# A hybrid encoder trunk on one core: the last pass of each attention score tile on 128 rows instead of 64, and a limit of nine on the fetched tiles of the state-space units

## The chip, the cores and the metric

One Trainium2 chip, one core of it. The metric is the device time of one launch in microseconds (us); lower is better. Engines are called by the profile's names: PE is TensorE (its matmuls), PEld its weight loads, DVE VectorE, ACT ScalarE, POOL GpSimd, SP SyncE, which only issues DMAs here.

## What is computed

Two post-norm layers on 512 tokens of 1024 channels, in f32. The even layer has a convolution branch (31 taps), a latent attention branch with 8 heads and a cross-attention branch; the odd layer has a state-space branch (S5, two directions, 64 groups of 16 channels) and a cross-attention branch. The part of the reference that the score tiles compute:

```python
def one_block(args):
    qn_b, qr_b = args
    s = (jnp.einsum('bqhd,bkhd->bhqk', qn_b, k_nope).astype(jnp.float32)
         + jnp.einsum('bqhr,bkr->bhqk', qr_b, k_rope).astype(jnp.float32)) * scale
    p = jax.nn.softmax(s, axis=-1).astype(v.dtype)
    return jnp.einsum('bhqk,bkhd->bqhd', p, v)
```

`q_rope` and `k_rope` have 64 components, `q_nope` and `k_nope` 128. The part that the state-space units compute, for each direction:

```python
bu_re = jnp.einsum('bsgc,gpc->bsgp', u, bb_re)
bu_im = jnp.einsum('bsgc,gpc->bsgp', u, bb_im)
_, _, x_re, x_im = lax.associative_scan(
    _cplx_combine, (a_re_seq, a_im_seq, bu_re, bu_im), reverse=reverse, axis=1)
return (jnp.einsum('bsgp,gcp->bsgc', x_re, c_re.astype(f32))
        - jnp.einsum('bsgp,gcp->bsgc', x_im, c_im.astype(f32)))
```

## The kernel before

**Numbers in two parts.** A large f32 operand is split into a high part (rounded by a cast on ACT) and a low part (the rest, by a subtraction on DVE), and a product is three matmul passes: high by high, low by high, high by low. Tiles of such parts are of the type float32r and lie in the arena `sr`; f32 tiles lie in `sb`, small ones in `sz`, PSUM is `ps`. A pass of 512 columns reads as `ps<-sr 128*128 128x512`, where the first pair is rows by columns of the weights.

**Heads (`mla_head`, L900).** Each of the eight heads makes four score tiles of 128 queries by 512 keys, each of five passes into one PSUM bank: three for the 128 components without rotary, two for the 64 rotary ones. For the rotary part the query tile `st` holds on 128 rows both the high part and the low part of the head's 64 rows (the even head has the high part on rows 0 to 63, the odd head on rows 64 to 127). `krh` and `krl` are the high and the low part of the rotary keys; both have the 64 keys' rows twice, on rows 0 to 63 and 64 to 127. So the fourth pass, `st` by `krh` on 128 rows, gives high by high and low by high at once. The fifth pass takes the high rows of `st` alone, by the same 64 rows of `krl` (L924, L934).

**Units (`s5_unit`, L1293).** Layer 1 has eight units of eight groups each. A unit fetches from DRAM its input `U` (128x512) and six tiles of 128x1024 words, in this order: two with its input matrices (`B`, L1304), one with rotations (`E`, L1305), two with output matrices (`C`, L1357) and one strip of the direct term (`Tt`, L1359). On PE come eight matmuls into halves of a bank (`64x256` below, the z passes; each reads in the trace as two), eight transposes (`128x128`), then 24 matmuls for the output (`64x128`): for each quarter two of the direct term and four by the states `X`. Between the transposes and the states DVE makes six products, four scans of 511 elements (`64x511`) and four products; POOL combines those into `X[0]` and `X[1]` (L1355, L1356). Between the units PE has the passes of other work: gates, the cross-attention's heads and, after the last, the matmuls of the gated unit and the output projection.

**The planner.** The program records every operation of both layers and then schedules them itself (`schedule`, L289), with costs for each instruction, due times by program order, and an allocator for the arenas and the PSUM banks (`alloc`, L361). The result is one fixed order for each engine. An operation is placed once its inputs are ready by the planner's costs and its tiles have room. `QUOTA` (L65) says how many tiles of a tag may live at once; a tag without an entry is limited by the arena alone (21504 words for `sb`). The tag of a `pair()` without a name is its line, so before the change the six fetched tiles of a unit all have the tag of L1298, with no entry. To a matmul the planner gives the same cost for the same columns, whatever its rows (L262):

```python
return 13.0 + on * 0.4175
```

All instructions are issued from one line, L535, so the trace is read by shape and arena.

Of the kernel before, what the change touches and what calls it, by code (L numbers as in the profile page):

```python
# [61 lines left out]

SB_WORDS = {"S": 21504, "R": 26624, "Z": 4864}
ENGINES = ("PE", "DVE", "ACT", "POOL", "SP")
QUOTA = dict(wr=3, wh=4, wl=4, wrv=1, whv=1, wlv=1, wrk=1, whk=1, wlk=1, A=4, S=3, T=2, R=1, Q=1, O=4, V=1, Z=2, W=2, Y=1, pr=6, bb=2, bt=2, nat=2, ncim=2, strips=2, qE=1, qt=2, qbt=1, qpw=1, qC=2, qB=1, C=2, D=1, cgl=2, U=2)  # L65
INF = float("inf")
NEAR, RESERVE = 30, dict(R=3584, S=2048)
RESERVEP = dict(R=4096, S=2560)
# [111 lines left out]
class Prog:  # L180
# [108 lines left out]
    def schedule(self):  # L289
# [71 lines left out]
        def alloc(o, near):  # L361
            done = []
            ok = True
            for x in o.tiles:
                if x.space == "D" or x.off is not None:
                    continue
                q = QUOTA.get(x.tag)
                if nxt.get(x.tag, 0) != x.idx or (q and live.get(x.tag, 0) >= q):
# [169 lines left out]
class Kernel:  # L538
# [361 lines left out]
    def mla_head(self, h):  # L900
        nc, A = self.nc, self.A
        if h % 4 == 0:
            self.v = self.mla_v(h // 4)
        wkn = self.wload(A["wkn"][h], 256, tag="k")
        ckv = [(t[0][:], t[1][:]) for t in self.ckv]
        cqa = lambda k: (self.cq[k][0][:], self.cq[k][1][:])
        ps = self.bank("A")
        self.mm3(ps[:], [self.wk(wkn, k) for k in range(2)], ckv)
        kh, kl = self.split(ps[:])
        ps = self.projF(A["wqn"][h], cqa, 6)  # L910
        qh, ql = self.split(ps[:])
        if h % 2 == 0:
            ps = self.projF(A["wqr"][h // 2], cqa, 6)
            r = self.rope(ps)
            self.stk = []
            for i in range(2):
                st = self.big(F32R)
                a, b = slice(i * 64, i * 64 + 64), slice((1 - i) * 64, (1 - i) * 64 + 64)
                nc.scalar.copy(st[a], r[a])
                nc.vector.tensor_tensor(st[b], r[a], st[a].bitcast(F32), op=ALU.subtract)  # L920
                self.stk.append(st)
        i = h % 2
        st = self.stk[i]
        rows = slice(i * 64, i * 64 + 64)  # L924
        scale = 192.0 ** -0.5
        pr = []
        for t in range(4):
            sl = slice(t * P, (t + 1) * P)
            s = self.bank("S")
            nc.tensor.matmul(s[:], lhsT=qh[:, sl], rhs=kh[:], start=True, stop=False)  # L930
            nc.tensor.matmul(s[:], lhsT=ql[:, sl], rhs=kh[:], start=False, stop=False)
            nc.tensor.matmul(s[:], lhsT=qh[:, sl], rhs=kl[:], start=False, stop=False)
            nc.tensor.matmul(s[:], lhsT=st[:, sl], rhs=self.krh[:], start=False, stop=False)
            nc.tensor.matmul(s[:], lhsT=st[rows, sl], rhs=self.krl[rows], start=False, stop=True)  # L934
            mx = self.sm(1, tag="mx")
            nc.vector.reduce_max(mx[:], s[:], axis=AX.X)
            p = self.big(F32, "pr")
            self.softmax_tail(s[:], p[:], scale, mx[:])
            pr.append(p)
        pt = []  # L940
        for k in range(4):
            tp = self.bank("T")
            for t in range(4):
                nc.tensor.transpose(tp[:, t * P:(t + 1) * P], pr[t][:, k * P:(k + 1) * P], self.ident[:])
            pt.append(self.split(tp[:]))
        o = self.bank("V")
        vs = slice((h % 4) * P, (h % 4) * P + P)
        self.mm3(o[:], [(v[0][:, vs], v[1][:, vs]) for v in self.v], [(a[:], b[:]) for a, b in pt])
        m = self.tmp()
        nc.sync.dma_start(out=m[:], in_=self.mgd[h][:])  # L950
        nc.vector.scalar_tensor_tensor(m[:], o[:], 0.5, m[:], op0=ALU.mult, op1=ALU.mult)
        return m
# [340 lines left out]
    def s5_unit(self, i):  # L1293
        nc, A = self.nc, self.A
        V, G = nc.vector, nc.gpsimd

        def load(src, t=None):
            t = t or self.pair()  # L1298
            nc.sync.dma_start(out=t[:], in_=src)
            return t  # L1300

        half = lambda t, x: t[:, x * N:(x + 1) * N]
        U = load(self.ud[i][:].rearrange("s (c n) k -> (s c) (n k)", n=8), self.big())
        B = [load(self.s5d[2 * i + h][0][:]) for h in range(2)]  # L1304
        E = load(self.rotd[i][:])  # L1305
        E = [half(E, x) for x in range(2)]

        zt = []
        for j in range(2):
            zp = self.bank("W")  # L1310
            for m in range(2):
                for h in range(2):
                    n = j * 4 + m * 2 + h
                    nc.tensor.matmul(zp[h * 64:h * 64 + 64, m * 256:m * 256 + 256].rearrange("p (x c) -> p x c", x=2),
                                     lhsT=U[:, n * 64:n * 64 + 64],
                                     rhs=B[j][:].rearrange("p (x c) -> p x c", x=2)[:, :, (n % 4) * P:(n % 4) * P + P],
                                     start=True, stop=True, skip_group_check=True)
            t = self.big()
            nc.scalar.copy(t[:], zp[:])
            zt.append(t)  # L1320
        Z = [self.bank("Z"), self.bank("Z")]
# [11 lines left out]
        t = [self.tmp() for _ in range(2)]  # L1333
# [6 lines left out]
        W = Z  # L1340
# [9 lines left out]
        t = [self.tmp() for _ in range(2)]  # L1350
# [6 lines left out]
        C = [load(self.s5d[2 * i + h][1][:]) for h in range(2)]  # L1357
# [3 lines left out]
        Y = self.bank("Y")  # L1361
# [262 lines left out]
```

## Time and profile before

| | |
|---|---|
| median of 3 runs | 1063.86 us (1058.15 to 1064.89) |
| the profiled execution | 1060.0 us, span 1058.2 us |
| mean granted TensorE clock | 0.979 |
| PE busy | 1007.6 us (95%), 5296 matmul records |
| PEld busy | 792.2 us (75%) |
| DVE busy | 799.2 us (76%) |
| ACT busy | 450.1 us (43%) |
| POOL busy | 514.7 us (49%) |
| DMA | 180.02 MB, mean 170 GB/s |

Times in the rows are microseconds from the start of the span; a row of a timeline merges neighbouring instructions of one kind, and names the shape of its first one. Matmuls are pipelined and their listed lengths overlap, so a matmul's pace is read from a run of them. "<-" names whose semaphore ended a wait. The stages: the even layer's projections up to about 355 us, the eight heads to about 553 (the convolution's taps on DVE run beside both), the even layer's output projection and the odd layer's first projections to about 690, the state-space units to about 875, then the gated unit and the last projection.

### The profile page before, as it was taken

To read this page: it belongs to the slowest core of one execution; us is meant where nothing else is said; L and a number is where in the kernel's file an instruction comes from. 1 tells how busy PE (TensorE), PEld (TensorE's weight loads), DVE (VectorE), ACT (ScalarE), POOL (GpSimd) and SP (SyncE) were. 2 spreads that over 40 slices of the span, in tenths; PEclk is the share of its full clock that TensorE was granted. 3 is DMA by queue.
4 is the path that set the end of the run, shared out by engine and by line. 5 is a ranking of instruction groups with operands and counts; after the bars stand their busy time and mean duration, and the time that the engine had idled before them with its cause. 6 is when DMAs were issued, how large, how long until landed. Compare 5 with 4: busy or idle time off the path is not lost. (4 is left out here: it accounts for less than half of the span.)

```text
span 1058.2 us, 15020 instructions
## 1 busy us (share of the span) xinstructions
PE 1007.6 (95%) x5296; PEld 792.2 (75%) x5296; DVE 799.2 (76%) x1285; ACT 450.1 (43%) x798; POOL 514.7 (49%) x741
## 2 busy tenths in 40 slices
PE   9999899999999999998799999999989979999996
PEld 7888788787788666665578888887767757888885
DVE  7787999999999898987896648517797695434346
ACT  5532455555323457475672223423436344422210
POOL 0557767788899988888699901000121011000001
PEclk9999999999999999998899999999999998999998
DMA  7433634325776454445398753883856633243413
GB/s 261 140 116 114 209 115 168 127 95 173 261 234 220 132 169 135 133 139 197 130 307 257 248 194 120 308 268 120 242 188 198 242 107 104 96 139 120 149 50 79
DMA packets 80171, 180.02 MB, mean 170 GB/s; under 512 B 24161, under 2 KB 28897, under 8 KB 80097
## 3 DMA queue, kind: packets, MB, share of 16 engines
q1 hardware_dynamic: 80096, 179.07, 51.9%
q8 instruction: 41, 0.67, 0.3%
q14 instruction: 34, 0.27, 0.1%
HBM read 142.93 MB, written 36.11 MB: 169 GB/s over the span
## 5 line engine op out<-in xcount | busy, mean ns | idle before, releaser
L535 PE MATMUL ps<-sr 128*128 128x512 f32 (+1 forms) x3904 | 925.5, 392 | 28.4 <-DVE sr L535 13.0
L535 PEld LDWEIGHTS ps<-sr 128*128 128x128 f32 x3904 | 709.9, 190 | 201.3 <-issue 21.7
L535 DVE TENSOR_TENSOR sr<-sb,sr 128x1024 fp32r<-128x1024 f32 (+4 forms) x230 | 270.1, 1186 | 172.4 <-ACT sr L535 130.2
L535 POOL TENSOR_TENSOR sb<-sb 128x512 f32<-128x512 f32 (+3 forms) x246 | 256.2, 1055 | 190.9 <-DVE sb L535 177.7
L535 ACT CAST sr<-sb 128x1024 fp32r<-128x1024 f32 (+4 forms) x230 | 200.7, 886 | 323.9 <-PE ps L535 187.2
L535 DVE SCALAR_TENSOR_TENSOR ps<-sb,sz,ps 128x503 f32<-128x503 f32 (+14 forms) x240 | 167.5, 736 | 0.0
L535 POOL TENSOR_TENSOR sz<-sz 128x64 f32<-128x64 f32 (+2 forms) x75 | 44.4, 596 | 221.6 <-DVE sz L535 218.2
L535 POOL TENSOR_TENSOR sb<-sb,sz 128x512 f32<-128x512 f32 (+4 forms) x160 | 131.8, 842 | 31.1 <-DVE sz L535 11.2
L535 ACT CAST sr<-ps 128x512 fp32r<-128x512 f32 (+1 forms) x100 | 55.8, 570 | 45.5 <-PE ps L535 45.2
L535 DVE TENSOR_TENSOR sr<-ps,sr 128x512 fp32r<-128x512 f32 (+1 forms) x100 | 65.3, 661 | 10.7 <-ACT sr L535 9.8
L535 ACT COPY sb<-ps 128x512 f32<-128x512 f32 (+3 forms) x78 | 40.8, 541 | 73.0 <-PE ps L535 51.9
L535 DVE SCALAR_TENSOR_TENSOR sb<-sb,ps 128x512 f32<-128x512 f32 x64 | 47.1, 739 | 29.6 <-ACT sb L535 12.5
L535 PE MATMUL ps<-sz,sb 128*128 128x128 f32 (+2 forms) x608 | 62.4, 237 | 4.1 <-DVE sr L535 1.8
L535 PE MATMUL ps<-sb 128*64 128x128 f32 (+2 forms) x768 | 58.4, 306 | 8.0 <-POOL sb L535 7.5
L535 PEld LDWEIGHTS ps<-sz,sb 128*128 128x128 f32 (+1 forms) x608 | 47.1, 131 | 20.8 <-ACT sb L535 6.8
L535 PEld LDWEIGHTS ps<-sb 128*64 128x64 f32 (+1 forms) x768 | 36.4, 131 | 33.3 <-POOL sb L535 13.1
L535 POOL TENSOR_TENSOR sb<-sz 64x64 f32<-64x64 f32 (+1 forms) x128 | 55.3, 440 | 4.9
L535 ACT ACTIVATE sb<-ps 128x512 f32<-128x512 f32 (+1 forms) x72 | 38.1, 548 | 41.1 <-PE ps L535 38.8
L535 ACT ACTIVATE sb<-ps,sz 128x256 f32<-128x256 f32 (+1 forms) x64 | 36.8, 580 | 18.6 <-DVE sz L535 13.6
L535 DVE TENSOR_TENSOR sb<-sb,ps 128x512 f32<-128x512 f32 x63 | 40.4, 680 | 2.0 <-PE ps L535 1.3
L535 DVE TENSOR_TENSOR_SCAN ps<-sb,ps 64x511 f32<-64x511 f32 x32 | 39.2, 1224 | 1.8 <-ACT ps L535 1.1
L535 ACT ACTIVATE sb<-sb,sz 128x512 f32<-128x512 f32 (+1 forms) x65 | 38.2, 622 | 5.3 <-DVE sz L535 5.2
(47 smaller groups left out, 338.9 us busy)
## 6 DMA issues: line engine op xcount, KB each, us to landing
sb<-w SPq DMA_DIRECT2D x70, 512.0 KB
sb<-scr SPq DMA_DIRECT2D x48, 512.0 KB
scr<-sb SPq DMA_DIRECT2D x40, 512.0 KB
sb<-scr SPq DMA_DIRECT2D x76, 256.0 KB
sb<-wo SPq DMA_DIRECT2D x32, 512.0 KB
scr<-sb SPq DMA_DIRECT2D x46, 256.0 KB
sb<-s5bt SPq DMA_DIRECT2D x16, 512.0 KB
sb<-wglu SPq DMA_DIRECT2D x16, 512.0 KB
```

What stands on the lines that cost most here:

```text
L535: o.ins = getattr(eng[o.eng], o.meth)(*[real(x) for x in o.a], **{k: real(v) for k, v in o.k.items()})
```

## The change

The fifth pass of each score tile runs on all 128 rows of `st` and `krl`. It so adds the product of the low parts, which the reference's full product contains too. And the fetched tiles of the units get a tag of their own, `un`, with an entry of nine in `QUOTA`.

```diff
-QUOTA = dict(wr=3, ..., cgl=2, U=2)
+QUOTA = dict(wr=3, ..., cgl=2, U=2, un=9)
...
         i = h % 2
         st = self.stk[i]
-        rows = slice(i * 64, i * 64 + 64)
         scale = 192.0 ** -0.5
...
             nc.tensor.matmul(s[:], lhsT=st[:, sl], rhs=self.krh[:], start=False, stop=False)
-            nc.tensor.matmul(s[:], lhsT=st[rows, sl], rhs=self.krl[rows], start=False, stop=True)
+            nc.tensor.matmul(s[:], lhsT=st[:, sl], rhs=self.krl[:], start=False, stop=True)
...
         def load(src, t=None):
-            t = t or self.pair()
+            t = t or self.pair("un")
             nc.sync.dma_start(out=t[:], in_=src)
             return t
```

Up to the middle of the units each engine's order is as before; from there on layer 1 is in another order on all five engines. In the rows below `128x512` is a pass of other work, `64x256` a z pass, `128x128` a transpose, `64x128` an output matmul (two of the direct term come first, then the states').

PE around the last unit, before: its z passes are done, its transposes are the row of eight, and the 20 outputs behind them belong to the unit before.

```order
L535 MATMUL ps<-sr 128x512 x19
L535 MATMUL ps<-sb 64x128 x2
L535 MATMUL ps<-sz,sb 128x128 x8
L535 MATMUL ps<-sr 128x512 x3
L535 MATMUL ps<-sb 64x128 x20
L535 MATMUL ps<-sr 128x512 x4
L535 MATMUL ps<-sb 64x128 x2
L535 MATMUL ps<-sr 128x512 x4
L535 MATMUL ps<-sb 64x128 x2
L535 MATMUL ps<-sr 128x512 x5
```

The same place now: the last of the unit's z passes, its two direct terms, its transposes, and its first state outputs behind the row of 53.

```order
L535 MATMUL ps<-sb 64x256 x4
L535 MATMUL ps<-sb 64x128 x2
L535 MATMUL ps<-sr 128x512 x8
L535 MATMUL ps<-sz,sb 128x128 x8
L535 MATMUL ps<-sr 128x512 x53
L535 MATMUL ps<-sb 64x128 x2
L535 MATMUL ps<-sr 128x512 x5
L535 MATMUL ps<-sb 64x128 x20
```

The outputs of the unit before the last now come ahead of the last unit's transposes, and the passes of other work between those and the first state output went from 3 + 4 + 4 to 53.

DVE in the last unit now: six products, with a split (`sr<-sb,sr`) among them, then the scans (the order lists a scan as SCALAR_TENSOR_TENSOR) and the four products.

```order
L535 TENSOR_TENSOR ps<-sb,ps 128x512
L535 TENSOR_TENSOR sb<-sb,ps 128x512
L535 TENSOR_TENSOR sr<-sb,sr 128x512
L535 TENSOR_TENSOR ps<-sb,ps 128x512
L535 TENSOR_TENSOR sb<-sb,ps 128x512
L535 TENSOR_TENSOR ps<-sb,ps 128x512
L535 SCALAR_TENSOR_TENSOR ps<-sb,ps 64x511
L535 TENSOR_TENSOR ps<-ps,sb 128x512
L535 SCALAR_TENSOR_TENSOR ps<-sb,ps 64x511 x3
L535 TENSOR_TENSOR sb<-sb,ps 128x512 x4
```

Before, the six products of the last unit stood together, as the trace shows them.

PE at the fifth and sixth unit now: the first row of 20 is the fifth unit's outputs, the z passes and the transposes are the seventh's, the other rows of `64x128` the sixth's.

```order
L535 MATMUL ps<-sb 64x128 x20
L535 MATMUL ps<-sr 128x512 x2
L535 MATMUL ps<-sb 64x128 x2
L535 MATMUL ps<-sr 128x512 x7
L535 MATMUL ps<-sb 64x256 x8
L535 MATMUL ps<-sz,sb 128x128 x3
L535 MATMUL ps<-sb 64x128 x2
L535 MATMUL ps<-sz,sb 128x128 x5
L535 MATMUL ps<-sr 128x512 x5
L535 MATMUL ps<-sb 64x128 x20
```

Rows of this form stood at the third and fourth unit before.

SP, the fetches of the fourth unit, the two orders' difference: `128x1x1024` is the strip, `w` a weight tile, `128x512` the next unit's input.

```order
 L535 DMA sb<-scr_3367 128x1024
 L535 DMA sb<-scr_3573 128x1024
+L535 DMA sb<-w 128x1024 x2
 L535 DMA sb<-scr_3622 128x1x1024
-L535 DMA sb<-w 128x1024 x3
-L535 DMA sb<-scr_5945 128x512
+L535 DMA sb<-w 128x1024
+L535 DMA sb<-scr_5942 128x512
```

The strip, the last of a unit's six tiles, went behind two weight tiles.

## Rows read from the trace of the kernel before

**Rows 1.** Stages: length, busy us of PE, PEld, DVE, ACT, POOL; PEclk, DMA share, GB/s

```profile
355.00:414.00 59.00, 55.67 (x305) 37.04 (x305) 52.43 (x101) 35.65 (x73) 50.30 (x69) 1.00 0.46 144
414.00:448.00 34.00, 31.66 (x179) 24.38 (x178) 32.63 (x46) 18.77 (x36) 29.07 (x34) 1.00 0.45 139
448.00:482.00 34.00, 30.02 (x177) 19.89 (x175) 28.07 (x58) 25.00 (x52) 30.93 (x42) 1.00 0.41 129
482.00:553.00 71.00, 61.16 (x291) 42.13 (x291) 58.44 (x91) 42.06 (x78) 57.01 (x70) 0.86 0.66 216
553.00:690.00 137.00, 136.47 (x730) 113.52 (x730) 85.11 (x99) 45.09 (x61) 59.73 (x63) 0.99 0.69 228
690.00:875.00 185.00, 173.56 (x1102) 131.58 (x1100) 133.74 (x189) 78.42 (x172) 22.20 (x24) 0.99 0.61 192
875.00:1058.00 183.00, 174.03 (x794) 143.61 (x794) 83.21 (x113) 50.01 (x72) 5.07 (x5) 0.97 0.34 107
```

**Rows 2.** Groups by shape, PE, whole span: count, busy us, mean ns, idle before

```profile
L535 PE MATMUL ps<-sr 128*128 128x512 f32 x3584 | 877.6, 399 | 26.8 <-DVE sr L535 11.8 <-DVE sb L535 7.1 <-ACT sb L535 4.5
...
L535 PE MATMUL ps<-sr 64*128 64x512 f32 x32 | 17.3, 542 | 0.0
```

**Rows 3.** Timeline of PE, three runs: start, length, shape of the first, count

```profile
339.82 10.13 PE L535 MATMUL ps<-sr 128*128 128x512 f32 x44
...
366.23 2.70 PE L535 MATMUL ps<-sr 64*128 64x512 f32 x8
...
495.33 6.68 PE L535 MATMUL ps<-sr 128*128 128x512 f32 x11 [1.15 <-DVE sr L535]
```

**Rows 4.** Groups by shape, PE, of 366.3:368.7, then of 495.4:501.4

```profile
L535 PE MATMUL ps<-sr 64*128 64x512 f32 x2 | 1.0, 494 | 0.0
...
L535 PE MATMUL ps<-sr 64*128 64x512 f32 x3 | 2.4, 791 | 0.0
```

**Rows 5.** Groups by shape, PE, of 355:414, then of 482:553

```profile
L535 PE MATMUL ps<-sr 64*128 64x512 f32 x16 | 7.9, 495 | 0.0
...
L535 PE MATMUL ps<-sr 64*128 64x512 f32 x8 | 5.4, 681 | 0.0
```

**Rows 6.** DVE's waits for PE in 355:414, 448:482, 482:553: us, times, longest

```profile
DVE sz L535 <- PE ps L535: 3.7, 7, 0.9
...
DVE sb L535 <- PE ps L535: 1.8, 2, 1.3
DVE sz L535 <- PE ps L535: 1.5, 1, 1.5
...
DVE sr L535 <- PE ps L535: 3.2, 2, 2.8
...
DVE sz L535 <- PE ps L535: 1.8, 4, 0.6
```

**Rows 7.** Timeline of PE at the last unit's first state outputs, waits in brackets

```profile
873.97 0.69 PE L535 MATMUL ps<-sb 128*64 128x128 f32 x4 [5.63 <-POOL sb L535]
875.05 2.50 PE L535 MATMUL ps<-sr 128*128 128x512 f32 x5 [0.39 <-DVE sr L535]
```

**Rows 8.** Busy time by stage, behind that wait

```profile
875.00:881.00 6.00, 5.95 (x39) 5.01 (x41) 0.00 (x0) 0.00 (x0) 1.12 (x1) 0.50 0.01 3
```

**Rows 9.** Timeline of DVE, the last unit's first product

```profile
862.61 0.70 DVE L535 TENSOR_TENSOR ps<-sb,ps 128x512 f32<-128x512 f32 x1
```

**Rows 10.** Timeline of PE at the third to fifth unit, waits in brackets

```profile
783.30 1.08 PE L535 MATMUL ps<-sb 128*64 128x256 f32 x8
784.92 1.08 PE L535 MATMUL ps<-sb 128*64 128x256 f32 x8 [0.53 <-DVE ps L535]
...
786.83 0.33 PE L535 MATMUL ps<-sz,sb 128*128 128x128 f32 x1 [0.46 <-DVE sb L535]
787.58 0.44 PE L535 MATMUL ps<-sb 128*64 128x128 f32 x4 [0.42 <-POOL sb L535]
```

**Rows 11.** Timeline of SP, fetches from DRAM scratch: start, length of the burst, count

```profile
776.63 4.92 SPq L535 DMA_DIRECT2D sb<-scr  x7
```

More of the change, by code (lines that the diff above doesn't have):

```diff
@@ L64 @@
 ENGINES = ("PE", "DVE", "ACT", "POOL", "SP")
-QUOTA = dict(wr=3, wh=4, wl=4, wrv=1, whv=1, wlv=1, wrk=1, whk=1, wlk=1, A=4, S=3, T=2, R=1, Q=1, O=4, V=1, Z=2, W=2, Y=1, pr=6, bb=2, bt=2, nat=2, ncim=2, strips=2, qE=1, qt=2, qbt=1, qpw=1, qC=2, qB=1, C=2, D=1, cgl=2, U=2)
+QUOTA = dict(wr=3, wh=4, wl=4, wrv=1, whv=1, wlv=1, wrk=1, whk=1, wlk=1, A=4, S=3, T=2, R=1, Q=1, O=4, V=1, Z=2, W=2, Y=1, pr=6, bb=2, bt=2, nat=2, ncim=2, strips=2, qE=1, qt=2, qbt=1, qpw=1, qC=2, qB=1, C=2, D=1, cgl=2, U=2, un=9)
 INF = float("inf")
```

## Prediction

> **What bounds the kernel now.** I read the busy time by stage first. From 553 us to the end PE is the bound: 136.47 of 137 us ahead of layer 1's state-space units, 173.56 of 185 us while they run, 174.03 of the last 183 [rows 1]. Before that, in the eight attention heads (355 to 553), PE is busy 55.67 of 59, 31.66 of 34, 30.02 of 34 and 61.16 of 71 us, and DVE nearly as long: 52.43, 32.63, 28.07 and 58.44 [rows 1]. There the two wait for each other. So PE can gain in two places: from passes in the heads that take longer than they need, and from the 11.4 us in which it stands in the units' stage (185 less 173.56). The change touches both: the score's last pass in the heads, and the number of fetched tiles in the units.
>
> **Edit 1, the last score pass on 128 rows.** 32 passes (8 heads, 4 query tiles) are on 64 rows. Their listed mean is 542 ns against 399 for a 128-row pass of the same 512 columns [rows 2], but listed times overlap, so I take whole runs. A run of 44 passes on 128 rows takes 10.13 us [rows 3]. Less the last one's own 0.40, that is 9.73 / 43 = 0.226 us a pass. A run of eight takes 2.70 us [rows 3] and holds two 64-row passes [rows 4]. Eight at the plain pace would take 7 x 0.226 + 0.40 = 1.98, so the two cost 0.72 more, 0.36 us each.
>
> From 482 to 553 the granted clock is 0.86 on the mean [rows 1], and a 64-row pass takes 681 ns on the mean against 495 in the first stage [rows 5]. A run of eleven there takes 6.68 us [rows 3], with three 64-row passes of 791 ns [rows 4]. At the lower of the two clocks the plain pace is 0.452, eleven take 4.97, and the overhang of a run's last pass (0.40 - 0.226 = 0.17, at most doubled) makes it 5.14 to 5.32. So three cost 1.36 to 1.54, and I take 0.50 each. Of the eight passes in this stage (681 - 495) / (791 - 495) = 0.63 are at the lower clock: five at 0.50 and three at 0.36, 3.6 us. The first 16 [rows 5] cost 16 x 0.36 = 5.8, the other eight, in the third stage, 2.9. The sum is 12.3 us of PE. After the edit each costs as much as its neighbours: nothing more is loaded or evicted, since both operands have 128 rows already.
>
> How much of it reaches the end? The order in the heads is unchanged on every engine, so DVE must come earlier too, and it can do so only by time in which it waited for PE. In the first stage its small operations waited 3.7 us for PE, against 5.8 saved; in the third 1.8 + 1.5 = 3.3 against 2.9; in the last 3.2 + 1.8 = 5.0 against 3.6 [rows 6]. In the second DVE is full (32.63 of 34 [rows 1]) and merely carries the shift on. So 3.7 + 2.9 + 3.6 = 10.2 is the most that I expect, and I take 9.0, which leaves 1.2 for waits that PE newly has for DVE. From 553 on PE is full, and what is gained stays gained. Bounds: 12.3 if DVE gives way everywhere, 3.6 if all of the first 24 passes' gain is eaten.
>
> What the rows show is that a pass on half the rows costs more than a whole one [rows 2 to 4]. The Trainium skill, "TensorE: Matmul & The Clock Gate", section "Part 2: What happens when you issue a matmul", says of the weight load that the row count does not matter, and of a stream of matmuls that its pace is set by the columns alone; by that edit 1 saves nothing, and the sum is edit 2 alone. The Trainium skill, "TensorEngine Tiling (Array Packing)", section "Tiling Modes", says that a change of tiling mode drains the engine; with that the trace agrees, at 0.36 us a pass.
>
> **Edit 2, at most nine fetched tiles.** No instruction is added on any engine. The planner places layer 1 anew from the middle of the units on, and two places count.
>
> The last unit. Before, between its transposes and its first state output PE has 3 + 4 + 4 passes of 512 columns and the unit before's outputs, and then stands 5.63 us for POOL and 0.39 for DVE [rows 7]. Right behind that the granted clock is 0.50 for 6.00 us, in which PE is busy 5.95 [rows 8]: half, 3.0 us, is lost. After, 53 passes stand there, 53 x 0.226 = 12.0 us. What they must cover is the unit's chain on DVE and POOL: from 862.61, DVE's first product [rows 9], to 873.97, when PE goes on [rows 7], 11.4 us. In the new order one more DVE operation on 128x512 stands within it, 0.70 by that first product's row [rows 9]. So 12.0 of cover for a chain of 12.1: I take 0.5 us of wait. Should the cover be gone, it costs up to those 12.1.
>
> The fifth and sixth unit now follow each other as the third and fourth did before, where PE stood 0.53 + 0.46 + 0.42 = 1.4 us [rows 10]. That place moves, and I cost the move at nothing. But the seventh unit's z passes, which stand between those two, come soon after its tiles are fetched, since only nine may be there. Before, the fifth unit was in that position: a burst of seven fetches was issued from 776.63 on [rows 11], and its z passes began at 783.30 with no wait ahead of the first [rows 10]. I take 1.0 us for the new place; the bounds are 0 and the whole of that stretch, 783.30 - 776.63 = 6.7 us. The weights' fetches, which SP issues in the same queue, now go partly ahead of a unit's strip tile; they are needed earlier, and I cost that at nothing, or at the same 6.7 if the strip is late.
>
> Sum of edit 2: 5.63 + 0.39 + 3.0 - 0.5 - 1.0 = 7.5. Bounds: 9.0 with no new wait; 9.0 - 6.7 - 6.0 = -3.7 with a late burst and two more falls of the clock at 3.0 each.
>
> **The sum.** 9.0 + 7.5 = 16.5 us. The profiled execution took 1060.0, so 1043.5. The median of the runs is 1063.9, 3.9 above that execution; against the median I expect 1047.4, given as 1047, or 1.6% faster. A change of 1%, 10.6 us, is about what a measurement of this kernel can tell from none.
>
> **Rivals.**
> Edit 1 is eaten: PE's shorter passes become PE's waits, because DVE has as little as 4% of slack. For it: DVE busy 32.63 of 34 us in the second stage [rows 1]. Against it: DVE's own waits for PE, 12.0 us in the rows named [rows 6]. Time: 1063.9 - 7.5 = 1056.4. That half the rows cost no more than all would end at the same number, and rows 3 and 4 leave it little. By the skill's rule on rows, above, it would be so.
>
> Edit 2 only moves the wait: the tight pair or the last unit's cover costs what was won. For it: 12.1 of chain against 12.0 of cover. Against it: 53 passes where 11 stood. Time: 1063.9 - 9.0 = 1054.9.
>
> Slower: with nine tiles a unit fetches only half of its successor's six ahead, so that fetches are late unit after unit. The place is each unit's first z pass; the price is a burst of 6.7 us [rows 10, 11] and the clock's 3.0 behind it [rows 8], 9.7 a unit. Two late units use up the gain (19.4 against 16.5), and three give 1063.9 - 16.5 + 29.1 = 1076.5. Against it: before, one unit's fetches were as late, without a wait, and DMA is busy only 0.61 of this stage [rows 1].
>
> **Chances.** Both terms as summed, 0.58 (own range 1041 to 1053). Edit 1 eaten, 0.14, and rows that cost nothing, 0.03. Edit 2 moved, 0.14. Slower by late fetches, 0.07. Neither gains, 0.04. Faster by over 1% (under 1053.2) is the first case and 0.08 of the two rivals that lie next to that border, 0.66; slower by over 1% is 0.07; within 1% the rest, 0.27. The range: at best 12.3 + 9.0 = 21.3, which is 1042.6 against the median and, as the fastest run shown lies 5.7 under it, some 1038; at worst 3 us of gain, 1061, which takes in the rivals next to the border and leaves the slow one out.
>
> **What would show it.** Edit 1 is right if no 64-row pass of 512 columns is left, runs in the heads go at 0.226 us a pass, and the stage that began at 553 begins some 9 us earlier. It is eaten if PE's waits in the heads grow by what its busy time falls. Edit 2 is right if PE's longest wait in the units is under 2 us and the granted clock stays at 1.00 through the last unit. It is wrong if PE waits over 3 us for a DMA, DVE or POOL at the z passes of the fifth or seventh unit or at any unit's state outputs. More than 1061 would mean that both terms failed, or that a new stall of over 10 us stands among the units.

## The result, and the profile after

The changed kernel takes 1051.70 us in the median of 3 runs (1050.03 to 1053.27), against 1063.86: a ratio of 0.9898, interval 0.9867 to 0.9929. Timed again beside 23 runs of the kernel before, it came to 0.9902 (0.9868 to 0.9936). It is faster by 1%, at the border that the forecast set between faster and the same: its first median lies 1.5 us below that border (1053.2), its second, 1055.29, 2.1 us above. The forecast was 1047 us, 1.6%.

The profiled execution took 1050.0 us, span 1048.2, which is 10.0 less than before. The trace was cut at the same instruction of PE as the kernel before at 355.6 and 552.7 us: the heads now take 191.2 us for 197.1 (6.0 less, before rounding), all that follows 501.5 for 505.5 (4.0 less), and what lies ahead is alike. The busy time by stage, cut to within half a microsecond where [rows 1] is cut (columns as there):

```profile
355.00:411.00 56.00, 51.58 (x305) 37.25 (x305) 53.15 (x102) 36.29 (x74) 51.25 (x69) 1.00 0.48 153
411.00:446.00 35.00, 32.81 (x176) 25.32 (x177) 32.81 (x45) 18.31 (x35) 28.78 (x34) 0.95 0.43 133
446.00:479.00 33.00, 28.46 (x179) 20.98 (x177) 27.75 (x59) 25.80 (x54) 31.36 (x44) 0.96 0.45 142
479.00:547.00 68.00, 56.16 (x290) 40.97 (x289) 58.43 (x89) 41.00 (x77) 55.11 (x68) 0.89 0.68 217
547.00:684.00 137.00, 136.34 (x729) 113.52 (x729) 84.28 (x99) 44.95 (x61) 59.75 (x63) 0.99 0.69 227
684.00:865.00 181.00, 173.09 (x1092) 129.99 (x1092) 127.72 (x181) 76.64 (x168) 20.53 (x22) 1.00 0.62 201
865.00:1048.00 183.00, 173.47 (x806) 142.37 (x804) 90.13 (x122) 51.70 (x77) 6.48 (x6) 0.99 0.33 104
```

The first stage is 3 us shorter, the second 1 longer at a clock of 0.95 where [rows 1] had 1.00, the third 1 shorter at 0.96 for 1.00, the fourth 3 shorter, the units 4. PE's largest group by shape over the whole span:

```profile
L535 PE MATMUL ps<-sr 128*128 128x512 f32 x3616 | 881.2, 398 | 30.1 <-DVE sr L535 12.5 <-DVE sb L535 8.3 <-ACT sb L535 4.6
```

and in PE's timeline the run of eight that [rows 3] has at 366.23:

```profile
364.99 2.10 PE L535 MATMUL ps<-sr 128*128 128x512 f32 x8
```

All 64-row passes of 512 columns are gone: 3584 + 32 = 3616. The run of eight takes 2.10 us for 2.70, 0.30 for each of its two. PE's idle time ahead of these passes rose from 26.8 [rows 2] to 30.1. PE's timeline at the last unit's first state outputs:

```profile
867.67 6.28 PE L535 MATMUL ps<-sr 128*128 128x512 f32 x27
874.54 0.44 PE L535 MATMUL ps<-sb 128*64 128x128 f32 x4 [0.59 <-POOL sb L535]
874.91 1.43 PE L535 MATMUL ps<-sr 128*128 128x512 f32 x5
```

and the busy time behind it:

```profile
876.00:882.00 6.00, 6.00 (x61) 5.08 (x60) 3.08 (x3) 2.25 (x5) 0.00 (x0) 1.00 0.60 186
```

The wait of 5.63 + 0.39 us [rows 7] is 0.59, and the clock behind it is 1.00 where [rows 8] had 0.50.

### The profile page after: what moved, and what is told of

It reads as the page before. It is cut to its first block, busy times and chain, and to the rows that moved or that the text cites. A ratio compares the mean times of both kernels' runs of the same rounds, so it can differ in the third digit from the quotient of the medians.

```text
span 1048.2 us, 15032 instructions
## 1 busy us (share of the span) xinstructions
PE 996.8 (95%) x5296; PEld 791.0 (75%) x5296; DVE 798.1 (76%) x1285; ACT 449.7 (43%) x798; POOL 514.1 (49%) x741
## 4 chain that ended last, share of the span: by engine, by line
PE 66%; DVE 18%; DMA 6%; ACT 5%; issue 3%; POOL 1%; SPq 1%; DVEq 0%; ACTq 0%; POOLq 0%
PE ps L535 66%; DVE ps L535 7%; DVE sr L535 7%; DVE sb L535 3%; DMA sb<-w 3%; ACT sb L535 2%; ACT sr L535 2%; DMA sb<-wo 1%; DVE sz L535 1%; DMA sb<-m0v 1%; POOL sb L535 1%; DMA sb<-m0k 1%; SPq L535 1%; DMA sb<-m1v 0%; DMA sb<-m1k 0%
## 5 line engine op out<-in xcount | busy, mean ns | idle before, releaser
L535 PE MATMUL ps<-sr 128*128 128x512 f32 (+1 forms) x3904 | 915.4, 390 | 32.3 <-DVE sr L535 14.4
L535 POOL TENSOR_TENSOR sb<-sb,sz 128x512 f32<-128x512 f32 (+4 forms) x160 | 132.6, 848 | 31.1 <-DVE sz L535 11.1
L535 DVE TENSOR_TENSOR sr<-ps,sr 128x512 fp32r<-128x512 f32 (+1 forms) x100 | 65.5, 661 | 10.9 <-ACT sr L535 10.3
L535 ACT COPY sb<-ps 128x512 f32<-128x512 f32 (+3 forms) x78 | 40.8, 542 | 60.3 <-PE ps L535 45.4
L535 PEld LDWEIGHTS ps<-sb 128*64 128x64 f32 (+1 forms) x768 | 34.3, 127 | 30.9 <-issue 14.5
```

Source lines behind the costliest of these rows:

```text
L535: o.ins = getattr(eng[o.eng], o.meth)(*[real(x) for x in o.a], **{k: real(v) for k, v in o.k.items()})
```

## Experiments

The stages below are cut in each trace at the same instructions as above, "heads" and "rest" (from the heads' end to the end of the span), each from one profiled execution. A row's ratio is to runs of the kernel before that were made beside it (medians of 1063.00 to 1063.86 us), and is not the quotient of two medians. Times up to the heads say nothing of the edits: their code is the same in all kernels, and they ran from 353.9 to 361.0 us over the profiles.

| kernel | median us | ratio to before (interval) | heads | rest |
|---|---|---|---|---|
| before | 1063.86 | 1 | 197.1 | 505.5 |
| changed | 1051.70 | 0.9898 (0.9867 to 0.9929) | 191.2 | 501.5 |
| changed, again | 1055.29 | 0.9902 (0.9868 to 0.9936) | 194.6 | 501.6 |
| 128 rows alone | 1054.23 | 0.9904 (0.9877 to 0.993) | 193.1 | 504.4 |
| nine alone | 1057.87 | 0.9956 (0.9936 to 0.9976) | 199.2 | 501.9 |
| two passes on 64 rows | 1058.91 | 0.9951 (0.9933 to 0.997) | 196.1 | 505.8 |
| 128 rows, limit ten | 1056.18 | 0.9933 (0.9907 to 0.9958) | 190.9 | 506.4 |
| 128 rows, limit eight | 1062.71 | 0.9984 (0.9964 to 1.0004) | 192.0 | 513.5 |
| 128 rows, reserve | 1050.96 | 0.9869 (0.9839 to 0.9899) | 190.9 | 503.6 |
| the same, again | 1049.51 | 0.9878 (0.9847 to 0.9909) | 190.1 | 499.8 |
| 128 rows, eight and reserve | 1058.76 | 0.9961 (0.9938 to 0.9984) | 192.4 | 506.9 |
| light maximum, 64 rows | 1063.96 | 1.0007 (0.9985 to 1.0028) | 198.9 | 506.2 |
| light maximum, 128 rows | 1053.40 | 0.9911 (0.988 to 0.9943) | 191.0 | 506.6 |
| changed, 19 cuts | 1061.62 | 0.9995 (0.9978 to 1.0012) | 191.2 | 512.4 |

### Each edit alone, and the changed kernel again

128 rows alone (the entry of nine is taken out again, which gives the order of before on every engine):

```diff
-QUOTA = dict(wr=3, ..., cgl=2, U=2, un=9)
+QUOTA = dict(wr=3, ..., cgl=2, U=2)
```

> The 128-row pass alone; every engine keeps the order of the kernel before. Theory: the two edits add, and what the profile of the changed kernel shows of the heads belongs to this edit alone. So the heads end 6 us earlier than before (near 546.7), layer 1 lasts as before (505.5 us from there), the span is near 1052, the ratio near 0.994. Rival 1: the heads' gain is set by where the lower clock falls, so that another execution of the same order gives anything from 4 to 9 us. Rival 2: the edits don't add, and this one alone gives the whole 10 us (span 1048) or none.

Nine alone (the order of the changed kernel):

```diff
+        rows = slice(i * 64, i * 64 + 64)
...
-            nc.tensor.matmul(s[:], lhsT=st[:, sl], rhs=self.krl[:], start=False, stop=True)
+            nc.tensor.matmul(s[:], lhsT=st[rows, sl], rhs=self.krl[rows], start=False, stop=True)
```

> The limit of nine alone, the last pass still on 64 rows; every engine has the order of the changed kernel. Theory: the heads end as before (552.7) and layer 1 is 4 us shorter (501.5), with no stall of 5 us at the last unit and no lower clock behind it, but with more short waits at the fifth to seventh unit; span near 1054, ratio near 0.996. Rival: the new order's waits at the seventh unit hang on when its fetches come; with the heads as slow as before, they fall otherwise, and the gain is 0 or up to 7.5.

> The changed kernel once more, beside the next three on the same chip. Theory: the heads take 191 to 193 us as in the three executions of this order so far, the rest 501.5 to 502; span 1047 to 1050. Rival: the rest's 4 us less than with the order before was chance of one execution; then it is 504 to 506 here.

The heads belong to edit 1, the rest to edit 2. The changed kernel's rest came out again as expected (501.6), but its heads, 194.6, and its span, 1054.4, lie above what was expected. PE's timeline at the last unit, first of 128 rows alone, then of nine alone:

```profile
868.98 0.70 PE L535 MATMUL ps<-sb 128*64 128x128 f32 x4 [5.63 <-POOL sb L535]
870.06 2.50 PE L535 MATMUL ps<-sr 128*128 128x512 f32 x5 [0.39 <-DVE sr L535]
```

```profile
882.35 0.44 PE L535 MATMUL ps<-sb 128*64 128x128 f32 x4 [0.58 <-POOL sb L535]
```

Without the limit the stall is there, to the hundredth; with it and the old passes it is gone. The rest is 501.5, 501.6 and 501.9 us in the three profiles with nine, and 504.4 to 506.6 in the six of kernels in which PE has the order of before (mean 505.8): edit 2 is worth 4.1 us. The heads are 197.1, 199.2 and 198.9 in the three kernels with the lone 64-row pass (mean 198.4; one of them has the light maximum below), and 190.1 to 194.6 in the ten profiles on 128 rows (mean 191.7): edit 1 is worth 6.7. The sum, 10.8, lies between the two measurements of the changed kernel (12.2 and 8.1 us between the medians). By the medians each edit alone gains 9.5 and 5.9, more than its stage shows; this difference lies in the part ahead of the heads or between executions, and was not settled. By the whole time 128 rows alone (0.9904) cannot be told from both edits together (0.9898 and 0.9902): that the limit of nine adds to the 128 rows rests on the stage and on nine alone (0.9956).

### Is it the row count, or the change between row counts?

The fourth pass, too, is put on the same 64 rows (the product of the low query part and the high keys is left out):

```diff
-            nc.tensor.matmul(s[:], lhsT=st[:, sl], rhs=self.krh[:], start=False, stop=False)
+            o = nc.tensor.matmul(s[:], lhsT=st[rows, sl], rhs=self.krh[rows], start=False, stop=False)
+            nc.touch(o, st[:, sl], False)
+            nc.touch(o, self.krh[:], False)
```

The two `touch` lines tell the planner that all rows are read, so that the order stays that of before.

> The kernel before with the fourth pass of each score tile, too, on the same 64 rows as the fifth (the product of the low query part by the high key part is left out); the order on every engine is that of before. If the cost of the 64-row pass is that of changing between 64 and 128 rows, two in a row cost what one did: the first is followed at about 0.23 us, only the change into and out of the pair costs, the time is that of before within 1 us. If a pass on 64 rows is dear by itself, by 0.19 us each, 32 more of them cost 6 us of PE and some 4 us of the span.

Twice as many 64-row passes did not take the same time within 1 us, as was expected of the theory of the change, but less: 0.9951, and in the heads 196.1 us, 1.0 less than the profile of before and 2.3 less than the mean of three. In the heads' order the row count changes 59 times, before 64 times. The theory stands by the steps. PE's timeline has one run of 23 passes that is the same in all kernels; here it is in the kernel before:

```profile
397.44 7.10 PE L535 MATMUL ps<-sr 128*128 128x512 f32 x23
```

with three passes on 64 rows among them:

```profile
L535 PE MATMUL ps<-sr 64*128 64x512 f32 x3 | 1.5, 498 | 0.0
```

the same run with two passes of each score tile on 64 rows:

```profile
396.57 6.46 PE L535 MATMUL ps<-sr 128*128 128x512 f32 x23
```

seven passes on 64 rows among them, six in a row:

```profile
L535 PE MATMUL ps<-sr 64*128 64x512 f32 x7 | 2.1, 420 | 0.0
```

and in the changed kernel, with none:

```profile
395.57 6.29 PE L535 MATMUL ps<-sr 128*128 128x512 f32 x23
```

The first eleven steps of this run, from one pass's start to the next one's, worked out from the trace's records (s: a pass on 64 rows):

```
before            0.34 0.47 0.43 0.43s 0.42  0.42s 0.43  0.43s 0.34 0.23 0.23
two on 64 rows    0.34 0.33 0.34s 0.23s 0.23s 0.23s 0.23s 0.32s 0.34 0.23 0.23
changed           0.34 0.52 0.34 0.24  0.23  0.23  0.23  0.23  0.23 0.23 0.23
```

A 64-row pass behind another one takes 0.23 us, what a 128-row pass takes behind its like. Where the two kinds alternate each step is 0.43, 0.20 more, whichever kind it is. At the ends of the six the same 0.2 is spread over two steps (0.33 and 0.34, 0.32 and 0.34). The price is that of the change, twice for each lone pass.

The records of the weight loads show what is lost there. Inside a run a pass's weights begin to load 0.23 us ahead of it, while the pass before it runs (changed: load at 397.23, its pass at 397.46). At a change both begin together (before: 398.69), so the load runs ahead no more. The loader's idle time with no listed wait behind it, over the whole span, before and then changed:

```profile
PEld ps L535 <- issue: 36.3, 130, 0.7
PEld ps L535 <- issue: 22.6, 83, 0.8
```

It stands 83 times for 130, where 64 changes between row counts are gone and ten between column counts have come (below). Why PE does not load ahead across a change is not shown.

With the rule of the Trainium skill, "TensorE: Matmul & The Clock Gate", "Part 2: What happens when you issue a matmul", that columns set the pace and rows do not, the trace agrees inside a run of one kind (0.23 for both). With that of the Trainium skill, "TensorEngine Tiling (Array Packing)", "Tiling Modes", that a change of mode drains the engine, it agrees at the step between kinds (0.43), if a pass on 64 rows is such a mode, which no run here shows.

### What ate part of edit 1: is it DVE's load?

The row maximum over half of the scores takes 8.5 us from DVE in the heads (32 times 683 less 418 ns), once with the old passes and once on 128 rows:

```diff
-        scale = 192.0 ** -0.5
+        scale = 192.0 ** -0.5 / 64
...
-            nc.vector.reduce_max(mx[:], s[:], axis=AX.X)
+            o = nc.vector.reduce_max(mx[:], s[:, 0:256], axis=AX.X)
+            nc.touch(o, s[:, 256:512], False)
+            o.cost = 64 + 1.043 * 512
```

The last two lines keep the order as it was. The maximum of the other half is left out, so the result is not the reference's.

> The kernel before (64-row pass, order of before on every engine) with less work for DVE in the heads: each of the 32 row maxima is taken over the first 256 of the 512 scores, and the softmax's scale is cut 64-fold so that nothing overflows. The left-out half of a maximum should save about 0.27 us each on DVE, 8.6 us in all. Theory (DVE and PE wait for each other in the heads): the heads, 196 to 199 us with the 64-row pass, end some 3 to 6 us earlier, for PE's waits for DVE shrink. Rival (the heads are set by PE's own passes and its lower clock alone): 196 to 199 stays.

> The same lighter maximum with the fifth score pass on 128 rows, same order. Theory (of the 9 to 12 us that the 32 passes save on PE, the missing 3 were eaten by waits for DVE): with DVE relieved, the heads end 8 to 10 us earlier than in the kernel with the light maximum and the 64-row pass, where with the full maximum the difference was 5 to 7 (191 to 193 against 196 to 199). Rival (the missing 3 us are PE's lower-clock stretches, which stay as long): the difference stays at 5 to 7.

The groups by shape of DVE in the heads, light maximum on 64 rows:

```profile
L535 DVE TENSOR_REDUCE sz<-ps 128x1 f32<-128x256 f32 x32 | 13.2, 418 | 10.1 <-PE ps L535 9.9
```

The first expectation fell: 8.5 us less of DVE's work gained nothing (198.9 us of heads, ratio 1.0007), and DVE only waits longer for PE, 9.9 us ahead of the maxima alone, where before it was 6.1. The maxima's share of DVE's load does not bound the heads. The second stayed undecided by its number: the difference between the pair is 7.9 us of heads, against 6.7 with the full maximum, and heads of one kernel differ by 3.4 between two profiles (191.2 and 194.6). Its theory fails by another: PE's idle time in the heads is 25.0 us with the light maximum on 128 rows, the longest of the ten profiles on 128 rows, so a lighter DVE did not shorten PE's waits in sum.

### Other limits, and room kept free instead of a limit

Ten and eight tiles, room for the main work in layer 1 without a limit, and eight with that room; all on 128 rows. The first pair of lines is the kernel with ten, the second stands in those with more room (the limit of eight is un=8, none un=99):

```diff
-QUOTA = dict(wr=3, ..., cgl=2, U=2, un=9)
+QUOTA = dict(wr=3, ..., cgl=2, U=2, un=10)
...
-RESERVE1 = dict(R=2048, S=512)
+RESERVE1 = dict(R=2048, S=2048)
```

> The changed kernel with a limit of ten instead of nine: PE, DVE and POOL keep the order of before, and only fetches are issued in another order. Theory: the gain of the limit comes from the new order on PE and DVE, not from the fetches; so this is like the 128-row pass alone, span near 1052, with the stall of 5.6 us at the last unit. Rival: the fetches themselves matter, by room in SBUF or by coming later; then PE waits for a DMA at z passes (slower than 1052), or the last unit's stall shrinks (faster).

> The changed kernel with a limit of eight. In its order PE has 18 passes of 512 columns between the last unit's transposes and its first state output (11 before, 53 with nine). Theory: what counts is that cover against a chain of some 11.4 us; 18 passes and the outputs among them are 6.7 us, so PE stands 4 to 5 us there and the clock falls behind it: rest 504 to 505, span near 1051. Rival: fewer tiles give more room, and room is what gains; then the rest is 501.5 or less, span 1048 or less.

> The changed kernel without a limit on fetched tiles, but with 2048 words of the arena (instead of 512) that the planner keeps free ahead of time in layer 1. Its order has 57 passes of 512 columns at the last unit and 28 at the sixth, where the limit of nine left 13. Theory: the gain comes from passes that stand ready to cover the last unit's chain, however the room for their weights is kept; so no stall at the last unit, rest 500 to 502, span 1046 to 1048. Rival: the number of fetched tiles itself matters (their DMA comes at another time); then without the limit the rest is 505 and the span near 1052.

> Limit of eight and a reserve of 2048 words together: 56 passes at the last unit and 40 at the sixth; only the fourth unit is left with 19. Theory: with one tight place in place of two, about 2 us less of waiting than the changed kernel: rest 499 to 500, span near 1046, ratio near 0.986. Rival: the waits only move again, by late fetches of the units' tiles, and the rest stays 501.5 or more.

> The version without a limit and with four times the room kept free for the main work in layer 1 (2048 words in place of 512), score pass on 128 rows, once more. Theory (it removes the last unit's stall as the limit of nine does, and its order has fewer waits): a median of 1049 to 1053, ratio 0.984 to 0.990 again, units to end 337 as before. Rival (its lead on the changed kernel, 1050.96 against 1055.29 in one call, was the chance of where the lower-clock stretches fell): 1053 to 1056, no better than the changed kernel.

Ten leaves PE's order as it was before, and the stall too (5.62 us at 870.20). Eight took far longer than its theory and its rival had it (a rest of 513.5 us, where 504 to 505 was expected). What PE waits for most from the units on, in all, times, longest, and then PE's timeline at the last unit, both with eight:

```profile
PE ps L535 <- ACT sb L535: 5.0, 5, 2.2
PE ps L535 <- POOL sb L535: 4.8, 4, 3.6
PE ps L535 <- DMA sb<-scr: 1.5, 2, 0.8
```

```profile
872.12 3.01 PE L535 MATMUL ps<-sr 128*128 128x512 f32 x8 [2.15 <-ACT sb L535]
878.76 0.69 PE L535 MATMUL ps<-sb 128*64 128x128 f32 x4 [3.63 <-POOL sb L535]
879.85 2.50 PE L535 MATMUL ps<-sr 128*128 128x512 f32 x5 [0.39 <-DVE sr L535]
```

The last unit's chain again has too little beside it: 2.15 + 3.63 + 0.39 = 6.17 us, and the passes behind it run at half pace. But the kernel before has as much there (6.02), so the 8 us by which eight is slower lie elsewhere: from the first unit on PE's listed waits are 15.2 us for 11.1, and its passes take 322.5 us for 318.7, in an order with 38 groups of 64-column passes for 32. Late fetches are not the cause with eight alone: the waits for DMA are 1.5 us in all. With eight and more room they are part of it. That kernel was expected near 1046 us with a rest of 499 to 500 and has 506.9, without a stall at the last unit; its waits moved, as its rival had it, in part to late fetches:

```profile
PE ps L535 <- DMA sb<-scr: 3.4, 3, 2.0
```

So it is not the number of tiles that helps, but what order the planner happens to find with it. The room kept free gets rid of the last unit's stall without a limit (no wait there is longer than 1.0 us). It took 1050.96 us where the changed kernel beside it took 1055.29, and 1049.51 when run again, without the changed kernel beside it. The intervals of the ratios overlap: that it beats the kernel before is shown, that it beats the changed one is not. Its rest differs by 3.8 us between its own two profiles; the first had a stretch of the lower clock at 764 that the second had not.

### What the units lost without a listed wait

PE's passes from the first unit on took 1.9 us more in the changed kernel than the sum of the prediction allows (below). Its order has 37 groups of 64-column passes between 128-column ones, where before it has 32. The test puts in 19 more, with the same passes: a 512-column pass that follows a state output's long run is moved into it.

```diff
-        order = self.schedule()
+        order = broken(self.schedule())
...
+            for m in (5, 10, 15):
...
+                    if (x.meth == "matmul" and not isy[nxt - 1] and x.a[0].n == 512 and x.a[0].shape[0] == P
+                            and all(at[p] <= a for p in x.preds)
+                            and x.k.get("start") is False):
+                        order.remove(x)
+                        order.insert(order.index(run[m - 1]) + 1, x)
```

> The changed kernel with one difference: in PE's order a 512-column pass that followed a state output's long run of 128 rows by 64 columns is put into that run, so that 19 more groups of 64-column passes stand between 128-column passes. The passes are the same ones, and every other engine's order is the same. Theory (each break between 128-column and 64-column passes costs PE a fixed time, which is what the change's five more groups cost): in the trace of the changed kernel a group of 4 passes of 128 columns between two 512-column ones takes 0.69 us and one of 40 takes 2.66, so 0.055 a pass and about 0.25 for the break; 19 x 0.25 = 4.7 us, so that from the first unit's products to the end it takes 340 us where both profiles of the changed kernel have 335.3, and a median near 1057 to 1059. Rival (the order in which the same passes stand costs nothing; the unlisted loss in the units is waits): 335 to 336.

From the first unit to the end it took 346.2 us, 10.9 more than the 335.3 of both profiles of the changed kernel; PE's idle time rose by 0.8 only. One such place in PE's timeline, in the changed kernel:

```profile
730.87 2.40 PE L535 MATMUL ps<-sb 128*64 128x128 f32 x40
733.20 1.42 PE L535 MATMUL ps<-sr 128*128 128x512 f32 x5
734.55 0.44 PE L535 MATMUL ps<-sb 128*64 128x128 f32 x4
```

and with three cuts (the two middle ones repeat the pattern):

```profile
732.11 0.87 PE L535 MATMUL ps<-sb 128*64 128x128 f32 x10
732.91 0.49 PE L535 MATMUL ps<-sr 128*128 128x512 f32 x1
...
735.79 0.87 PE L535 MATMUL ps<-sb 128*64 128x128 f32 x10
736.59 0.73 PE L535 MATMUL ps<-sr 128*128 128x512 f32 x2
737.25 0.44 PE L535 MATMUL ps<-sb 128*64 128x128 f32 x4
```

The same 40 and 5 passes take 734.55 - 730.87 = 3.68 us whole and 737.25 - 732.11 = 5.14 cut: 0.49 for each cut. Over all 19 it is 10.9 / 19 = 0.57, of which the idle time is 0.04. The weight loader's idle time from the first unit on, with no listed wait behind it, before, changed, and with the cuts:

```profile
PEld ps L535 <- issue: 8.7, 37, 0.7
PEld ps L535 <- issue: 10.8, 43, 0.8
PEld ps L535 <- issue: 18.9, 81, 0.8
```

The 19 cuts make 38 changes more, and the loader stands 38 times more, 8.1 us in all. The theory stands in its direction; its price of 0.25, from a short group's 0.69 us, was half of what a cut in the long run costs. A break between weights of 64 and of 128 columns costs PE time, as one between 64 and 128 rows does.

## Why the prediction was right or wrong

**Direction and sum.** Faster, inside the range, through the two edits named. The gain was 10.0 us between the two profiles (6.0 + 4.0), where the sum had 16.5 (9.0 + 7.5): both terms were taken too large. That the first median fell on the forecast's side of the 1% border is luck, since the second fell on the other. The range's lower end was reckoned wrong, 1042.6 - 5.7 being 1036.9 and not 1038, which changes nothing here. Of the rivals none holds: edit 1 is not eaten whole, edit 2 does not only move the wait, rows that cost nothing are refuted by 128 rows alone (0.9904), and the slow case by late fetches does not occur at nine; the most that PE waited for fetches from the first unit on was 3.4 us in all, with eight and more room.

**Edit 1, the price.** Right. I took 0.36 us a pass, 12.3 in all, from two runs. Taken apart at the same instructions (worked out from the records), PE's time in the heads was, as passes + idle:

| stage of [rows 1] | before | changed |
|---|---|---|
| 355 to 414 | 56.0 + 2.9 | 51.6 + 3.9 |
| 414 to 448 | 31.6 + 2.2 | 33.2 + 2.2 |
| 448 to 482 | 30.3 + 4.0 | 27.7 + 4.5 |
| 482 to 553 | 60.3 + 9.8 | 56.2 + 11.8 |
| heads | 178.2 + 18.9 | 168.7 + 22.5 |

The three stages with 64-row passes gave 4.4, 2.6 and 4.1, 11.1 us in all, against 5.8, 2.9 and 3.6 forecast. Over all profiles, the ten on 128 rows against the three with the lone 64-row pass, the heads' passes fell by 11.8 us in the mean (180.6 to 168.8).

**Edit 1, what reaches the end.** This step failed in its size: "10.2 is the most that I expect, and I take 9.0, which leaves 1.2 for waits that PE newly has for DVE". From 12.3 I took off 3.3; the profile takes off 5.1 from 11.1. PE's idle time grew by 3.6, and the second stage, where nothing was removed, lost 1.6 to the clock. PE's timeline there, and the busy time behind the wait:

```profile
427.97 8.24 PE L535 MATMUL ps<-sr 128*128 128x512 f32 x28 [2.01 <-DVE sr L535]
```

```profile
428.50:432.00 3.50, 3.50 (x10) 2.68 (x9) 3.50 (x7) 0.00 (x0) 2.02 (x7) 0.52 1.00 340
```

The wait of 2.01 us is as long as before at the same instruction, yet this time the clock is at its lower level behind it. It is not a fixed effect: in the changed kernel's second profile the clock does not fall there, and the second stage takes 33.7 us, as before. The waits are the firmer part: over the same ten and three profiles PE's idle time in the heads grew by 5.1 us in the mean (17.8 to 22.9), where the prediction took off 3.3. The idle time grew where PE meets a chain that does not start with its own passes. Near the end of the heads, before and then changed:

```profile
513.15 2.80 PE L535 MATMUL ps<-sr 128*128 128x512 f32 x5 [3.38 <-DVE sb L535]
517.73 1.65 PE L535 MATMUL ps<-sr 128*128 128x512 f32 x3 [1.78 <-ACT sb L535]
```

```profile
506.56 2.19 PE L535 MATMUL ps<-sr 128*128 128x512 f32 x5 [4.06 <-DVE sb L535]
511.39 2.08 PE L535 MATMUL ps<-sr 128*128 128x512 f32 x4 [2.64 <-ACT sb L535]
```

Two waits took back 1.5 us of what had been won. Over the ten and the three profiles these two grew by 1.8 us in the mean, two at about 383 and 387 by 1.9, and one at about 452 by 1.0 (instants of the trace before); with that most of the 5.1 has its place. DVE's waits for PE in the heads fell from 14.5 us to 8.2, by 6.3, hardly more than the heads gained; I had counted on 9 to 10. What stands ahead of the two waits can be read. DVE, before and then changed, and ACT:

```profile
507.77 5.33 DVE L535 SCALAR_TENSOR_TENSOR sb<-sb,sz,ps 128x512 f32<-128x512 f32 x8
501.17 5.33 DVE L535 SCALAR_TENSOR_TENSOR sb<-sb,sz,ps 128x512 f32<-128x512 f32 x8
```

```profile
515.95 1.04 ACT L535 CAST sr<-sb 128x1024 fp32r<-128x1024 f32 x1 [7.08 <-DMA sb<-wo]
509.61 1.04 ACT L535 CAST sr<-sb 128x1024 fp32r<-128x1024 f32 x1 [7.60 <-DMA sb<-wo]
```

The first wait ends with a row of eight operations on DVE, 5.33 us in both; the second ends with ACT's work behind its cast of a weight tile, which itself waits for that tile's fetch. From the row's start to the end of the second wait it is 9.96 us before and 10.22 after: PE's shorter passes shorten nothing there. The light maximum does not touch this either, and the first wait is 4.06 us with it too. So what DVE could give was counted from its waits for PE, where here a fixed row of its own work and a fetch set the end. Whether another order of these eight or an earlier fetch would give the rest was not tried.

**Edit 2, the stall.** Right: 6.02 us became 0.59, against 0.5 taken, and the clock behind it stays at 1.00. Right too the seventh unit's z passes: taken at 1.0, bounded by 6.7, they wait 0.37 us for a fetch and go on:

```profile
824.11 1.08 PE L535 MATMUL ps<-sb 128*64 128x256 f32 x8 [0.37 <-DMA sb<-scr]
825.81 1.08 PE L535 MATMUL ps<-sb 128*64 128x256 f32 x8 [0.62 <-DVE ps L535]
...
827.73 0.33 PE L535 MATMUL ps<-sz,sb 128*128 128x128 f32 x1 [0.46 <-DVE sb L535]
828.48 0.44 PE L535 MATMUL ps<-sb 128*64 128x128 f32 x4 [0.42 <-POOL sb L535]
```

**Edit 2, the order at no cost.** This failed twice. "That place moves, and I cost the move at nothing": the tight pair is at the new place, as the rows above show (0.62 + 0.46 + 0.42 = 1.50), but waits stayed at the old one as well:

```profile
781.23 1.08 PE L535 MATMUL ps<-sb 128*64 128x256 f32 x8 [0.78 <-DVE ps L535]
783.08 2.37 PE L535 MATMUL ps<-sr 128*128 128x512 f32 x9 [0.77 <-DVE sr L535]
```

Before, 1.4 us stood in one place [rows 10]; now 1.50 and 1.55 stand in two. And "no instruction is added on any engine" was taken to mean that the passes take what they took. From the first unit to the end PE's time was 318.7 + 11.5 (passes + idle) and is 317.6 + 8.5, with 9.2 us behind its last pass in both. Of the idle time the last unit's stall gave 5.4 and other waits took back 2.4; of the passes, where the clock was to give 3.0, only 1.1 came. The 1.9 between them is what five more groups of 64-column passes cost at 0.4 each; a price of this size is shown by the cuts (0.57) and by short groups in the trace (0.25 to 0.40), the weight loader's idle time, shown above, rose by 2.1 us, which fits; that the breaks are the whole of the 1.9 is worked out and not shown. So 5.4 + 1.1 - 2.4 = 4.1 us, where 7.5 was summed.

## What to carry to other kernels

On PE count the changes of shape in the order, not only the passes: a lone pass on half the rows among whole ones costs two changes of up to 0.2 us on top of its own 0.23, more than the same pass on all rows, and six such passes in a row cost only the two changes at their ends. When a planner's limit is moved, the stall that goes is read exactly from the trace, but the new order must be read for its small waits and its breaks as well, and a neighbouring limit must be tried before the number itself is believed (nine gains 4 us, ten nothing, eight loses 8). What an engine saves upstream of a chain that another engine sets reaches the end only in part: here 6 of 11 us.

## What had not been expected of the hardware

Half-row passes run at the same 0.23 us as whole ones once they follow each other, and a kernel with twice as many of them was 0.5% faster than the one before (0.9951, interval 0.9933 to 0.997), not slower. At each change of shape the weight load stops running ahead of its pass, with no wait listed. A 512-column pass put into a long run of 64-column passes costs 0.5 us besides its own 0.23, with no wait listed ahead of any of them. And where the lower clock falls differs between executions of the same kernel: the changed kernel's heads took 191.2 us in one profile and 194.6 in the other, with the same order on every engine.
